# A hybrid mLSTM / attention layer on one core: key loads a unit earlier, input scaling on another engine, slots and operand planes moved

## The chip, the core and the metric

The kernel runs on one core of one Trainium2 chip. Its engines work side by side, each through its own queue in order: TensorE (PE, with its weight loads as PEld), VectorE (DVE), ScalarE (ACT), GpSimd (POOL) and SyncE (SP), which here issues nearly all DMAs. Instructions of different engines wait for each other through semaphores. The metric is the device time of one execution in microseconds, as a median of runs.

## What is computed

One encoder layer on x of 2048 tokens by 1024 channels, in f32. It is, cut to what matters:

```
h = rmsnorm(x, g_mix);  z = h @ w_in
split z: qk_m, v_m, o_m, i, f | q, k, v of the neighbourhood attention | q_mem | gate_pre
h_m   = mLSTM in both directions over (silu(conv(qk_m)), v_m, i, f), summed, normed, times sigmoid(o_m)
h_na  = attention of each of 32 x 64 grid points to its 8 x 16 neighbours, with a bias table
h_mem = attention to 256 memory tokens
y     = sum over branches of sigmoid(gate) * (branch @ w_proj)
x     = x + y @ w_out
x     = x + relu(rmsnorm(x, g_ffn) @ w_up)^2 @ w_down
```

## The kernel before

**Precision.** A product in f32 is made of three matmuls: each operand is split into a high and a low plane, and high x high, high x low and low x high are summed (`mm3`, lines 241 to 243). ACT writes the high plane and DVE the low one: L185 and L186 for weights, L447 and L448 for inputs, L1365 and L1366 for the gates' operands.

**Blocks, groups, ticks.** Phase 1 walks four blocks (0 to 3) of 512 tokens. `block_a` runs the groups of one block in order: q and k of the neighbourhood attention; its v with q_mem; the convolved mLSTM q and k (4 groups); mLSTM v (4 groups); in blocks 1 and 2 four early gates; the output gate o (4 groups); in block 3 eight more gates. A group is 24 matmuls of 128x512, and after every 6 of them `tick()` runs: it takes one job off a list and advances the side streams by a step. The neighbourhood attention (`na_stream`), the memory attention and the q/k normalisation are such streams, so that their small matmuls lie between the large ones. TensorE's order is that of the program, written out by hand. The order of the other queues is made by a planner from priorities, which follow the program order; an instruction traced at `cur_priority + LATER` (60) counts as if it came later.

**Next block's inputs.** While one block is at work, `prep_x` loads a tile of 128 tokens of the next (already transposed, `xT`) and scales it by the gain `gmix` (a column for each of 8 slices) and by the reciprocal norms `rb` (a row), in eight DVE instructions (L428). `trans_x` then queues two jobs that split the tile into the planes of `hT`. There are two buffers for such tiles (tag `xt`). They are shared with `rms_x`, which loads the next block for its norms, and with `sums_down`.

**Sums of the down weights.** `sums_down` loads two 512 KB tiles of weights, makes four differences on DVE (L606) and stores them. There are 16 of these. `SUMS_1` says how many are made in each block of phase 1; the rest are made in `pair_gates`, in phase 3.

**Neighbourhood attention.** Its work is cut into units (group of query rows g, heads hg, half), each of four scores. `na_unit` fetches one: with half 0 it loads keys and queries in six DMAs (tiles `nak` and `naq`, two buffers each), with half 1 it uses the same ones. A score (`na_scores`) is one matmul (L1115), a minimum over scores and bias on DVE (L1118), the exponential on ACT (L1120), a reciprocal (L1122) and a scaling (L1123) on DVE, and a zero fill of the tile's end on POOL (L1126). Some ticks later TensorE transposes it (`na_transpose`, L1134), and after four heads `na_values` (L1148) multiplies with v. The tile for the scores has three buffers. The line that decides when a unit is fetched is:

```
            if todo and not fetched and (cur is None or cur["h"] > 0):
                last = self.na_unit(*todo.pop(0), last, 4 if cur else 8)
```

**Phase 2** runs the remaining gates of blocks 3 and 0 as 24-matmul groups, and the mLSTM (`ml_stream`) between them by ticks. Its 32 chunks (two directions in turn) start one in each slot; a slot has 3 or 4 ticks. From slot 16 on a chunk also adds the other direction's output, normalises, multiplies by the output gate and is transposed (L936 to L956). `load_raw` reloads the raw inputs of blocks 1 and 2 at a fixed gate.

**Phase 3** begins with the gates that are left when the mLSTM stream has ended. Beside them, one job a tick, `gate_operands` forms sums of the raw inputs (L1371) and splits them into planes (`X`). `pair_gates` then makes the remaining gates of blocks 1 and 2 in pairs, seven products for eight, followed by the merge, the output projection and the MLP in the same scheme.

Of the kernel before, what the change touches and what calls it, by code (L numbers as in the profile page):

```python
# [14 lines left out]
F32R = mybir.dt.float32r  # L15
BF16 = mybir.dt.bfloat16
AF = mybir.ActivationFunctionType
ALU = mybir.AluOpType
# [7 lines left out]
LOW, LATER, LATER_A, SOON = 100, 60, 60, 40  # L26
# [2 lines left out]
PAD = 256  # L29
EV = {1: 2, 2: 2, 3: 8}  # L30
XT = 2
PREP_V = 2
MEM_T, MEM_R = 6, 3
NA_LATER, NA_VALUES, NA_HOLD = {1: 5, 2: 5, 3: 4}, {1: 3, 2: 3, 3: 2}, 3
NAB = 4
# [4 lines left out]
NB = S // TB  # L40
# [6 lines left out]
SPILL = [0]  # L47
NA_AT = {1: (3,), 2: (1, 3), 3: (1, 2, 3)}
NA_RATE = {0: 1, 1: 2, 2: 2, 3: 2}
SUMS_1 = {0: 1, 1: 2, 2: 2, 3: 6}  # L50


def units(g):
# [31 lines left out]
class Body:  # L85
# [330 lines left out]
    def prep_x(self, gsrc=None, xt=None):  # L416

        if self.xorder:
            nc = self.nc
            b, t = self.xorder.pop(0)  # L420
            r0 = b * TB + t * 128
            if b == 0:
                self.xhs.append((self.load_norm(self.a["x"][r0:r0 + 128], self.gbc, gsrc, xt), t, False))
                return
            xt = self.x_tile(self.a["xT"][4 * b + t]).rearrange("p (k t) -> p k t", k=8)
            rb = self.rb[:, t * 128:(t + 1) * 128]
            for k in range(8):
                nc.vector.scalar_tensor_tensor(xt[:, k], xt[:, k], self.gmix[:, k:k + 1], rb, ALU.mult, ALU.mult)  # L428
            if b in GATES_3:
                self.store(self.scr["raw"][b][:, :, t * 128:(t + 1) * 128], xt)  # L430
            self.xhs.append((xt, t, True))
# [70 lines left out]
    def block_a(self, b):  # L502


        nc, a = self.nc, self.a
        hT = self.hT
        w = self.take(4)
        for i, t in enumerate(ORDER_0 if b == 0 else range(4)):
            if i == 0 or b == 0 and i < 3:
                self.trans_x()  # L510
            if b == 0 and i == MEM_R:
                self.mem_rms()
            p = self.tok_group(hT, w, t)
            z = self.t("zna", [128, 512], 4)
            nc.scalar.activation(z, p, AF.Copy)
            self.qkq.append(self.na_qk(b, t, z.rearrange("p (a b) -> p a b", b=32)))
        if b + 1 < NB:
            rms = self.rms_x(b + 1)
            self.jobs += [lambda: next(rms, None), None] * 10
        if b in SPILL:  # L520
            for k in range(8):
                self.jobs += [lambda k=k: self.store(self.scr["hT"][b][:, :, k], hT[:, :, k].bitcast(F32)), None]
        w = self.take(4)
        zif = self.t("zif", [128, 4, 16], 1)
        for t in range(4):
            p = self.tok_group(hT, w, t, slice(0, 256), 4)
            s = self.ev()[:, 0:256]
            nc.scalar.activation(s, p, AF.Copy)

            for half in range(2):  # L530
                for r in range(2):
                    p0 = r * 64 + half * 24
                    self.store(self.scr["vna"][half, 8 * b + 2 * t + r], s[p0:p0 + 40])
            self.done.add(("v", 4 * b + t))
            p = self.tok_group(hT, w, t, slice(256, 528), 4)
            z = self.t("zm", [128, 256], 4)
            nc.vector.tensor_copy(z, p[:, 0:256])
            nc.scalar.activation(zif[:, t], p[:, 256:272], AF.Copy)  # L538
            self.memq.append(self.mem_unit(b, t, z))
        self.jobs += [None, None, lambda: self.if_rows(b, zif)]  # L540
        if b == NB - 1:
            self.na_rate = 3
            self.mem_lanes[1] = (0,)
        gml = self.gbc[:, b % 2 * TB:(b % 2 + 1) * TB]
        sums, n = None, SUMS_1[b]

        def sum_step():
            nonlocal sums, n
            if sums is None and n:
                sums, n = self.sums_down(self.down_q.pop(0), self.x_tiles), n - 1  # L550
            sums = sums and next(sums, None) and sums

        for c in range(4):
            if c % 2:
                sum_step()
            self.conv(b, c, self.ch_group(self.take(1)[0], hT))
        w = self.take(4)
        for t in range(4):
            if t == PREP_V and b + 1 < NB and b not in GATES_3:
                self.prep_x()  # L560
            p = self.tok_group(hT, w, t)
            s = self.ev()
            nc.scalar.activation(s, p, AF.Copy)
            self.store(self.scr["v"][b][t * 128:(t + 1) * 128], s)
            if b == NB - 1:
                sum_step()
        if b in GATES_3:
            for j in range(EARLY):
                if j == EARLY - 2:
                    self.prep_x()  # L570
                self.gate(b, j)
                if j < 2:
                    sum_step()
        nc.sync.dma_start(gml, a["g_mlstm"])
        w = self.take(4)
        for t in range(4):
            if t:
                self.trans_x()
            if t < 3:
                self.prep_x()  # L580
            p = self.tok_group(hT, w, t)
            s = self.ev()
            nc.scalar.activation(s, p, AF.Tanh, scale=0.5)
            nc.vector.scalar_tensor_tensor(s, s, 1.0, gml, ALU.add, ALU.mult)
            self.store(self.scr["og"][b][t * 128:(t + 1) * 128], s)
        if b == NB - 1:
            for j in range(FIRST_3):
                if j == 2:
                    self.ml_logsig()
                self.gate(b, j)  # L590
                sum_step()
# [69 lines left out]
    def ml_stream(self):  # L661


        rows = self.ml_rows(0)
        for tick in range(START_2):
            if tick >= ROWS_2:
                next(rows, None)
            yield
        slot = 0
        dirs = [list(range(16)), list(range(15, -1, -1))]  # L670
        live = [[], []]
        when = {0: [3, 2], 1: [1], 2: [], 3: [3, 1, 2, 1, 2, 3, 1, 0]}
        d = 0
        while any(dirs) or any(live[0]) or any(live[1]):
            c = dirs[d].pop(0) if dirs[d] else None

            ticks = 3 if slot < 20 or slot >= 32 else 4
            if slot % 8 == 2 and slot < 24:
                rows = self.ml_rows(slot // 8 + 1)
            slot += 1  # L680
            live[d] = [None if c is None else self.ml_chunk(d, c)] + live[d][:3]
            for tick in range(ticks):
                for age in when[3 if tick == ticks - 1 else tick]:
                    if age < len(live[d]) and live[d][age]:
                        next(live[d][age], None)
                if tick < ticks - 1:
                    next(rows, None)
                yield
            if len(live[d]) == 4:
                live[d][3] = None  # L690
            d = 1 - d
# [310 lines left out]
    def na_stream(self):  # L1002
# [6 lines left out]
        while True:  # L1009
            if self.na_wait and self.na_tiles(self.na_wait[0]) <= self.done:  # L1010
                hold += 1
                if hold > NA_HOLD:
                    hold, g = 0, self.na_wait.pop(0)
                    todo += [(g, hg, half) for hg in range(2) for half in range(2)]
            if todo and not fetched and (cur is None or cur["h"] > 0):
                last = self.na_unit(*todo.pop(0), last, 4 if cur else 8)
                fetched.append(last)
                biases += [(last, h) for h in range(4)]
# [56 lines left out]
    def na_unit(self, g, hg, half, before, wait):  # L1075
# [2 lines left out]
        u = dict(g=g, hg=hg, half=half, nk=nr * 40, pts=[], h=0, wait=wait)  # L1078
        u["qk"] = before["qk"] if half else self.na_load_qk(g, hg, kr0, nr)
        u["kts"] = [(3 * i, min(3, nr - 3 * i)) for i in range((nr + 2) // 3)]  # L1080
        u["ho"] = before["ho"] if half else self.t("nho", [128, 2, 256], 1, F32R)
        u["bias"] = []
        self.na_v.append(u)
        self.na_load_v()
# [56 lines left out]

    def na_values(self, u):
        nc = self.nc
        g, hg, half, ho, kts, pts = (u[x] for x in ("g", "hg", "half", "ho", "kts", "pts"))
        po = self.ps("mx")[:, 0:128]
        for j, (r0, n) in enumerate(kts):
            for h in range(4):
# [148 lines left out]
    def phase_3(self):  # L1296
# [14 lines left out]
        nc.sync.dma_start(self.gbc, a["g_ffn"])  # L1311
        if self.raw is None:
            self.late_gates(lambda: self.raw is None)
        self.jobs += self.gate_operands()
        self.late_gates(lambda: True)
        while self.jobs:
            self.tick()
# [37 lines left out]
    def gate_operands(self, late=False):  # L1355
# [5 lines left out]
        def split(x, src):  # L1361
            for k in (0, 2):
                def job(k=k):
                    hi, lo = (X[x][:, l, k:k + 2] for l in range(2))
                    nc.scalar.activation(hi, src[:, k:k + 2], AF.Copy)  # L1365
                    nc.vector.tensor_tensor(lo, src[:, k:k + 2], hi.bitcast(F32), ALU.subtract)  # L1366
                jobs.append(job)

        def op(out, x, y, how):
# [19 lines left out]
    def pair_gates(self, b0, b1, mix1):  # L1389
# [19 lines left out]
        for n, j in enumerate(pairs):  # L1409
# [14 lines left out]
            add(u3, u2, c21)  # L1424
            add(p5, u3, p5)
            out(p5, c2, j + 1)
            if sums:
                next(sums.pop(0), None)
            product(w, c12, "s4", "b22", False)
            add(u3, u2, c12)  # L1430
            out(u3, c2, j)
# [5 lines left out]
            if slots is None:  # L1437
                while self.jobs:
                    self.tick()
                slots = self.p_h.tile([128, 4, 2, 1024], F32, name="sG", tag="hT", bufs=1)  # L1440
            for _ in range(1 + (n == 0)):
                if self.down_q:
                    q = self.down_q.pop(0)
                    load = lambda q, s=slots[:, q % 4]: self.sums_load(q, s)
# [328 lines left out]
```

## Time and profile before

| | us |
|---|---|
| median of 3 runs | 2931.28 |
| lowest and highest run | 2923.46, 2934.57 |
| profiled execution | 2925.4 |
| its span, first to last instruction | 2923.7 |
| PE, PEld busy | 2850.3, 2348.0 |
| DVE, ACT, POOL busy | 2086.1, 1219.6, 216.8 |

All later numbers of the trace are from the profiled execution. Times of day, as "at 354", are microseconds from the start of the span. A line of a timeline gives start, duration, engine, line of the kernel, operation, output<-inputs, shapes and, in brackets, how long the engine had been idle before it and what ended that. A line of a table by group gives the count, then busy time, the mean duration in ns, and the idle time before. The granted clock is the share of TensorE's full rate.

### The profile page before, as it was taken

Reading aid. Unit: us, or ns where it says so; the run is one execution under the profiler, and the core shown is the slowest. Engines: PE = TensorE matmul, PEld = TensorE weight load, DVE = VectorE, ACT = ScalarE, POOL = GpSimd, SP = SyncE. Lnnn points to the kernel's source line nnn. Section 1 sums busy time; section 2 is a strip of 40 time slices with the busy share of each in tenths; the row PEclk is TensorE's granted clock in tenths of the full one; section 3 lists DMA queues with packets and bytes.
Section 4 is the critical chain, followed back from the end, with each engine's and each line's share of the span. In section 5 each row is a group of like instructions: output and inputs, shape, how many; then the busy total and the mean of one; then the engine's idle time right before and its main releaser. Section 6 shows DMA issues by size and latency. Waiting matters only on the chain.

```text
span 2923.7 us, 41742 instructions
## 1 busy us (share of the span) xinstructions
PE 2850.3 (97%) x14908; PEld 2348.0 (80%) x14908; DVE 2086.1 (71%) x3586; ACT 1219.6 (42%) x2326; POOL 216.8 (7%) x382
## 2 busy tenths in 40 slices
PE   8999999998999989999999999999999999999999
PEld 7787787787777768888888888888888888888887
DVE  5768768787645668657598888566786988885666
ACT  6556556455443445442243334533312433344331
POOL 4130030120012320000000000000000000000000
PEclk9999999999999999999999999999999999999999
DMA  7877968878887895738344446756864444466554
GB/s 263 252 246 224 288 210 256 270 224 253 282 273 250 275 321 195 274 112 267 123 142 155 154 159 206 246 189 222 308 200 125 141 158 146 154 241 212 190 191 160
DMA packets 341488, 625.42 MB, mean 214 GB/s; under 512 B 29120, under 2 KB 150912, under 8 KB 340768
## 3 DMA queue, kind: packets, MB, share of 16 engines
q1 hardware_dynamic: 341280, 622.76, 65.3%
q8 instruction: 117, 1.92, 0.3%
q14 instruction: 91, 0.75, 0.1%
HBM read 446.03 MB, written 176.62 MB: 213 GB/s over the span
## 4 chain that ended last, share of the span: by engine, by line
PE 83%; DVE 6%; DMA 6%; issue 2%; ACT 2%; SPq 1%; POOL 1%; DVEq 0%; ACTq 0%; POOLq 0%
PE mm L241 26%; PE mm L243 25%; PE mm L242 25%; DVE ws L186 1%; PE tr L1134 1%; DMA nak<-s_ks 1%; ACT ws L185 1%; PE pn L903 1%; PE mx L1148 1%; PE mx L1115 1%; DVE cy L711 1%; DMA wr<-in_w_units_dram 1%; DMA wb<-s_w 0%; PE mm L1536 0%; PE pn L906 0%
## 5 line engine op out<-in xcount | busy, mean ns | idle before, releaser
L241 PE MATMUL mm<-X,ws 128*128 128x512 f32 x1032 | 401.8, 389 | 0.0
L243 PE MATMUL mm<-X,ws 128*128 128x512 f32 x1032 | 401.5, 389 | 0.0
L242 PE MATMUL mm<-X,ws 128*128 128x512 f32 x1032 | 401.5, 389 | 0.0
L211 ACT ACTIVATE ws<-wr 128x512 fp32r<-128x512 f32 x294 | 176.8, 628 | 280.6 <-PE mm L243 181.7
L186 DVE TENSOR_TENSOR ws<-wr,ws 128x1024 fp32r<-128x1024 f32 (+1 forms) x160 | 196.7, 1236 | 84.5 <-ACT ws L185 79.1
L243 PE MATMUL mm<-X 128*128 128x512 f32 x616 | 239.7, 389 | 0.0
L242 PE MATMUL mm<-X 128*128 128x512 f32 x616 | 239.6, 389 | 0.0
L241 PE MATMUL mm<-X 128*128 128x512 f32 x616 | 239.6, 389 | 0.0
L241 PE MATMUL mm<-ws,hT 128*128 128x512 f32 (+2 forms) x640 | 233.6, 365 | 5.3 <-ACT zif L538 2.9
L243 PE MATMUL mm<-ws,hT 128*128 128x512 f32 (+2 forms) x640 | 226.8, 354 | 1.9 <-DVE hT L448 1.9
L242 PE MATMUL mm<-ws,hT 128*128 128x512 f32 (+2 forms) x640 | 226.1, 353 | 0.2 <-DVE ws L186 0.2
L243 PEld LDWEIGHTS mm<-X,ws 128*128 128x128 f32 x1032 | 193.7, 188 | 40.2
L242 PEld LDWEIGHTS mm<-X,ws 128*128 128x128 f32 x1032 | 193.7, 188 | 40.2
L241 PEld LDWEIGHTS mm<-X,ws 128*128 128x128 f32 x1032 | 193.8, 188 | 40.0
L185 ACT ACTIVATE ws<-wr 128x1024 fp32r<-128x1024 f32 (+1 forms) x160 | 168.3, 1058 | 103.3 <-PE mm L243 88.6
L212 DVE TENSOR_TENSOR ws<-wr,ws 128x512 fp32r<-128x512 f32 x294 | 198.2, 688 | 1.4
L1658 ACT ACTIVATE X<-X 128x1024 fp32r<-128x1024 f32 x109 | 115.7, 1062 | 198.2 <-DMA X<-s_t 79.2
L1659 DVE TENSOR_TENSOR X<-X 128x1024 fp32r<-128x1024 f32 x109 | 133.0, 1223 | 74.6 <-ACT X L1658 74.2
L1685 DVE TENSOR_TENSOR acc<-acc,mm 128x512 f32<-128x512 f32 x192 | 126.5, 684 | 65.4 <-PE mm L243 65.3
L241 PE MATMUL mm<-hT,ws 128*128 128x512 f32 x384 | 157.2, 409 | 0.7 <-ACT ev L626 0.7
L243 PE MATMUL mm<-hT,ws 128*128 128x512 f32 x384 | 150.6, 392 | 0.0
L242 PE MATMUL mm<-hT,ws 128*128 128x512 f32 x384 | 150.4, 392 | 0.0
(310 smaller groups left out, 6240.8 us busy)
## 6 DMA issues: line engine op xcount, KB each, us to landing
wr<-in_w_units_dram SPq DMA_DIRECT2D x276, 512.0 KB
s_s<-u SPq DMA_DIRECT2D x32, 1024.0 KB
s_g<-ev SPq DMA_DIRECT2D x96, 256.0 KB
ev<-s_g SPq DMA_DIRECT2D x96, 256.0 KB
s_a<-u SPq DMA_DIRECT2D x96, 256.0 KB
X<-s_s SPq DMA_DIRECT2D x45, 512.0 KB
nab<-in_rpb_dram SPq DMA_DIRECT2D x96, 220.0 KB
X<-s_a SPq DMA_DIRECT2D x32, 512.0 KB
```

The costliest lines, as they stand in the source:

```text
L185: nc.scalar.activation(w[:, 0], raw, AF.Copy)
L186: nc.vector.tensor_tensor(w[:, 1], raw, w[:, 0].bitcast(F32), ALU.subtract)
L211: nc.scalar.activation(hi, src, AF.Copy)
L212: nc.vector.tensor_tensor(lo, src, hi.bitcast(F32), ALU.subtract)
L241: mm(out, lhs[0], rhs[0], start=first, stop=False)
L242: mm(out, lhs[0], rhs[1], start=False, stop=False)
L243: mm(out, lhs[1], rhs[0], start=False, stop=last)
L711: nc.vector.scalar_tensor_tensor(y, z[:, k:k + n], self.cw[:, c, k:k + 1], y, ALU.mult, ALU.add)
L903: mm(pn[h % 2][:, h // 2], pt[:, h], v1[:, h], start=h < 2, stop=first)
L1658: nc.scalar.activation(hi, src, AF.Copy)
L1659: nc.vector.tensor_tensor(lo, src, hi.bitcast(F32), ALU.subtract)
L1685: nc.vector.tensor_tensor(c, c, p, ALU.add)
```

## The change

Six things, most of them one line each.

- **Keys.** A unit is fetched also when one is in hand already, if another is running; and when none is in hand, at once. The output tile `nho` is made in `na_values` instead of with the unit.
- **Scaling.** `prep_x` uses two GpSimd instructions over the whole tile of 128x1024 instead of eight on DVE.
- **When tiles are prepared.** In block 0 before value groups 0 and 2 (before: 2 only); in blocks 1 and 2 before early gates 0 and 2 (before: 2 only). In the output-gate groups the remaining two are jobs behind the split jobs of groups 1 and 2 (before: calls ahead of groups 0, 1 and 2).
- **Sums.** Blocks 1 and 2 make one each (before: two). `pair_gates` makes seven instead of five: up to two a pair in the first three pairs.
- **mLSTM slots.** Three ticks in slots 0 to 15 and from 32 on, four in 16 to 31 (before: three up to 19).
- **Operand planes.** `gate_operands` begins four empty jobs later, and its splits are traced at a priority 60 later.

```
-PREP_V = 2
+PREP_V = (0, 2)
-SUMS_1 = {0: 1, 1: 2, 2: 2, 3: 6}
+SUMS_1 = {0: 1, 1: 1, 2: 1, 3: 6}
...
-            for k in range(8):
-                nc.vector.scalar_tensor_tensor(xt[:, k], xt[:, k], self.gmix[:, k:k + 1], rb, ALU.mult, ALU.mult)
+            for y in (self.gmix.unsqueeze(2), rb.unsqueeze(1)):
+                nc.gpsimd.tensor_tensor(xt, xt, y.to_broadcast([128, 8, 128]), ALU.mult)
...
-            if t == PREP_V and b + 1 < NB and b not in GATES_3:
+            if t in PREP_V and b + 1 < NB and b not in GATES_3:
                 self.prep_x()
...
-                if j == EARLY - 2:
+                if j % 2 == 0:
                     self.prep_x()
                 self.gate(b, j)
-                if j < 2:
-                    sum_step()
...
             if t:
                 self.trans_x()
-            if t < 3:
-                self.prep_x()
+                if t < 3:
+                    self.jobs.append(self.prep_x)
...
-            ticks = 3 if slot < 20 or slot >= 32 else 4
+            ticks = 3 if slot < 16 or slot >= 32 else 4
...
-            if todo and not fetched and (cur is None or cur["h"] > 0):
+            if todo and (not fetched or len(fetched) == 1 and cur):
...
-        u["ho"] = before["ho"] if half else self.t("nho", [128, 2, 256], 1, F32R)
...
-        g, hg, half, ho, kts, pts = (u[x] for x in ("g", "hg", "half", "ho", "kts", "pts"))
+        g, hg, half, kts, pts = (u[x] for x in ("g", "hg", "half", "kts", "pts"))
+        if half == 0:
+            self.nho = self.t("nho", [128, 2, 256], 1, F32R)
+        ho = self.nho
...
-        self.jobs += self.gate_operands()
+        self.jobs += [None] * 4 + self.gate_operands()
...
+                    prio = self.tc.cur_priority
+                    self.tc.cur_priority = prio + LATER
                     nc.scalar.activation(hi, src[:, k:k + 2], AF.Copy)
                     nc.vector.tensor_tensor(lo, src[:, k:k + 2], hi.bitcast(F32), ALU.subtract)
+                    self.tc.cur_priority -= LATER
...
-            if sums:
-                next(sums.pop(0), None)
+            for _ in range(1 + (n < 3)):
+                if sums:
+                    next(sums.pop(0), None)
...
-            for _ in range(1 + (n == 0)):
+            for _ in range(1 + (n < 3)):
```

## The prediction

> **What bounds the kernel now.** I read the busy times first, then stretches of the span, then who TensorE waited for, then the timeline at each wait. In the stretches the columns are the length, then busy time and instructions of PE, PEld, DVE, ACT and POOL, the granted clock, the DMA share and GB/s.
>
> ```profile
> span 2923.7 us, 41742 instructions
> PE 2850.3 (97%) x14908; PEld 2348.0 (80%) x14908; DVE 2086.1 (71%) x3586; ACT 1219.6 (42%) x2326; POOL 216.8 (7%) x382
> ...
> 546.00:776.00 230.00, 219.07 (x1564) 179.02 (x1564) 170.11 (x419) 125.45 (x288) 32.52 (x76) 0.99 0.84 252
> ...
> 946.00:1000.00 54.00, 48.97 (x310) 38.96 (x309) 37.43 (x78) 21.70 (x83) 17.36 (x28) 1.00 0.81 247
> 1000.00:1142.50 142.50, 127.22 (x702) 103.65 (x701) 97.23 (x166) 66.89 (x209) 32.42 (x49) 0.95 0.85 280
> 1142.50:2917.00 1774.50, 1773.30 (x7880) 1467.33 (x7879) 1301.75 (x1814) 632.73 (x896) 0.00 (x0) 1.00 0.55 187
> ```
>
> TensorE sets the end. From 1142.5 on, where the MLP and the paired gates lie, it idles 1774.50 - 1773.30 = 1.2 us: nothing is to be had there, and anything added there that DVE or the DMA can absorb is free. The other idle time lies before 1142.5. The change adds and removes no matmul, so it can only act on these gaps and on what a gap does to the clock: the granted clock is 0.95 in 1000 to 1142.5, where 15.3 us are idle, and 1.00 behind it. I price a gap with its clock loss. Over the whole span 2923.7 - 2850.3 = 73.4 us are idle, so no edit to waiting can bring more than that and the clock.
>
> **The keys.** An attention unit is four scores (L1115); two units share one set of keys, loaded by six DMAs. Before, a unit is fetched when the current one has made a score and none is in hand. These four scores are each the first on a new set of keys; the bracket is TensorE's idle time and what the profile blames.
>
> ```profile
> 340.49 0.44 PE L1115 MATMUL mx<-nak,naq 96*128 96x440 f32 x1 [2.27 <-issue]
> 670.11 0.64 PE L1115 MATMUL mx<-nak,naq 96*128 96x440 f32 x1 [4.44 <-DMA nak<-s_ks]
> 700.63 0.44 PE L1115 MATMUL mx<-nak,naq 96*128 96x440 f32 x1 [1.48 <-DMA nak<-s_ks]
> 749.01 0.38 PE L1115 MATMUL mx<-nak,naq 96*128 96x320 f32 x1 [1.25 <-DMA cz<-s_fg]
> ```
>
> Then the last key DMA of the set used at 670.11, and the stretch around it:
>
> ```profile
> 662.38 0.31 SPq L1072 DMA_DIRECT2D nak<-s_ks  x1
> ...
> 650.00:675.00 25.00, 19.83 (x149) 15.29 (x146) 13.97 (x42) 10.75 (x27) 0.96 (x6) 0.93 1.03 294
> ```
>
> Two of the four have another label, but all fall on the first score of a pair of units, so I count them as the same wait: 2.27 + 4.44 + 1.48 + 1.25 = 9.44 us. The clock adds (1 - 0.93) x 25 = 1.75 us in the stretch that holds the largest. The last key DMA of that set was issued at 662.38 and the score began at 670.11, 7.7 us later, with the DMA engines full (1.03). After the change the fetch happens when one unit is in hand and another runs, so the load starts while the first unit of the pair before runs, not the second: more than one unit, five scores, sooner. 670.11 and 700.63 are the first scores of two sets that follow each other, eight scores in 30.5 us or 3.8 each, so the lead grows by an estimated 19 us, four times the largest wait. Two key tiles exist; the one needed was freed a score earlier, so SP shouldn't stand at these DMAs. V and bias loads keep their own counters, and the output tile moves to the values step. I take all of it: **-11.2 us** (bounds: -11.2, and 0 if the DMA engines are the limit, below).
>
> **The scaling on GpSimd.** Twelve token tiles are scaled. Before: eight DVE instructions each; after: two POOL passes over 128x1024.
>
> ```profile
> L428 DVE SCALAR_TENSOR_TENSOR xt<-xt,gmix,gbc 128x128 f32<-128x128 f32 x96 | 27.1, 347 | 9.2 <-DMA xt<-in_xT_dram 9.2
> L972 POOL TENSOR_TENSOR zna<-zna,rs 128x512 f32<-128x512 f32 x16 | 18.3, 1145 | 1.3
> L1233 POOL TENSOR_TENSOR zm<-zm,rs 128x256 f32<-128x256 f32 x18 | 13.5, 752 | 1.4
> ```
>
> One wait of TensorE in DVE's order of work, the same later, and all waits of this kind (total, times, longest):
>
> ```profile
> 351.46 1.65 DVE L428 SCALAR_TENSOR_TENSOR xt<-xt,gmix,gbc 128x128 f32<-128x128 f32 x6
> 353.62 1.23 DVE L186 TENSOR_TENSOR ws<-wr,ws 128x1024 fp32r<-128x1024 f32 x1 [0.52 <-ACT ws L185]
> 354.77 0.61 DVE L428 SCALAR_TENSOR_TENSOR xt<-xt,gmix,gbc 128x128 f32<-128x128 f32 x2
> 355.29 1.22 DVE L186 TENSOR_TENSOR ws<-wr,ws 128x1024 fp32r<-128x1024 f32 x1
> 356.43 0.45 DVE L1123 TENSOR_SCALAR nsb<-nsb,sm 128x440 f32<-128x440 f32 x1
> ...
> 363.40 2.19 DVE L428 SCALAR_TENSOR_TENSOR xt<-xt,gmix,gbc 128x128 f32<-128x128 f32 x8
> ...
> PE tr L1134 <- DVE nsb L1123: 6.2, 3, 2.2
> ```
>
> The stretches that hold the three waits:
>
> ```profile
> 350.00:375.00 25.00, 20.90 (x140) 16.60 (x142) 22.14 (x57) 15.05 (x30) 1.96 (x7) 0.93 0.96 318
> 525.00:550.00 25.00, 22.45 (x158) 17.93 (x157) 17.97 (x52) 11.96 (x24) 0.66 (x5) 0.95 0.90 294
> ```
>
> DVE is freed of 27.1 us. At 356.43 the softmax scaling (L1123), on which the transposes L1134 wait, stands behind eight L428 and two L186; from 363.40 eight L428 run in one piece before the next. The third wait, in 525 to 550, I read the same way. Eight take 1.65 + 0.61 = 2.26 us, over the longest wait of 2.2, so all 6.2 us go. Clock: (1 - 0.93) x 25 + (1 - 0.95) x 25 = 3.0 us. **-9.2 us**; bounds: 0 if L186 or a late load keeps L1123 late, -9.2.
>
> POOL gains 24 passes. From 752 ns at 256 columns and 1145 at 512, 1.54 ns a column: an estimated 1145 + 512 x 1.54 = 1.93 us a pass, 46 us in all on an engine that is 7% busy. A tile takes 3.9 us in place of 2.26, so 1.6 us later. Two of a block's four tiles now start much earlier (first and third value group, or first and third early gate), and the two sums dropped from blocks 1 and 2 no longer hold their buffers. The other two are emitted in the output-gate group, each two token groups ahead of its split into planes: ACT may stand there, and behind it PSUM evictions. For the three block changes that is six tiles at 0 to 1.6 us: 0 to 9.8; I take the middle, **+4.8 us**, as nothing here shows POOL in that place.
>
> **mLSTM slots.** Slots 16 to 19 get a fourth tick each, six more gate matmuls. TensorE's work is unchanged; gates only move. I match these slots with the stretch just before 946, and the idle time comes after: 54.00 - 48.97 = 5.0 us in 946 to 1000, where second-half chunks load saved scores and old outputs. More time per slot lets their loads keep up. Bounds -5.0 to +5.0 (a shift can as well move a wait); I take **-2 us**.
>
> The largest wait of all is later:
>
> ```profile
> PE tr L951 <- DVE h L947: 16.5, 8, 7.3
> ```
>
> It falls beside the reload of the raw inputs (128 x 8192 floats, 4 MB). That reload comes at a fixed gate; the slot's phase there is the same, one slot earlier, so I leave it at 0, but keep a gain for a rival.
>
> **Operand planes and sums.** The stream ends four ticks, one gate, later, so phase 3 starts one gate nearer to its first product on X.
>
> ```profile
> 1118.04 3.91 ACT L1365 ACTIVATE X<-raw 128x1024 fp32r<-128x1024 f32 x4 [1.97 <-DMA s_g<-ev]
> ...
> 1139.39 2.36 DVE L1366 TENSOR_TENSOR X<-raw,X 128x1024 fp32r<-128x1024 f32 x2
> ...
> 1142.52 0.39 PE L241 MATMUL mm<-X,ws 128*128 128x512 f32 x1
> ```
>
> Before, splitting started when X's space came free (1118.0) and the last plane was ready at 1141.8, 0.8 us ahead of the first product; that plane is used by the third. A matmul of the last stretch above takes 1774.5 / 7880 = 0.225 us, so a product of 12 takes 2.7 us, and that plane's slack is 0.8 + 5.4 = 6.2 us. A gate is 24 matmuls, 5.4 us. So one gate later it fits by 0.8 us; the cover is thin. Lower priority lets weights pass first. Bounds 0 to 5.4; I take **+1.4 us**. The two sums moved behind 1142.5 cost DVE eight instructions of 128x512 (0.68 us for that form, below) and 4 MB of DMA (eight tiles of 512 KB) where TensorE idles 1.2 us: 0.
>
> **Sum:** -11.2 - 9.2 + 4.8 - 2 + 1.4 = -16.2 us against the profiled execution's 2925.4 (span 2923.7 and 1.7 around it). The median of three runs is 2931.28, 5.9 above that execution; the same difference from it gives **2915 us**.
>
> **POOL beside DVE.**
>
> ```profile
> 1035.58 1.09 POOL L855 TENSOR_SCALAR_AFFINE_SELECT de<-de 128x512 f32<-128x512 f32 x1
> 1036.10 1.11 DVE L936 TENSOR_TENSOR h<-h,hf 128x512 f32<-128x512 f32 x1
> ...
> 1103.03 0.68 DVE L936 TENSOR_TENSOR h<-h,hf 128x512 f32<-128x512 f32 x1
> ```
>
> The same DVE form took 0.68 us alone and 1.11 beside a POOL pass, 0.43 more. The Trainium skill, SBUF — State Buffer, "Who interferes with whom", says that a DVE instruction with two SBUF inputs and a GpSimd one that reads SBUF exclude each other for the whole instruction, whichever comes first; the row agrees in sign, and by that rule a pass of 1.93 us could hold DVE for all of it.
>
> **Rivals.**
> 1. *The transfers are the limit.* DMA share is 1.03 at 650 to 675 and 0.96 at 350 to 375; earlier keys push weights and biases back, and TensorE waits for these. For: that share. Against: the stretch around has 0.84. The 11.2 us stay: 2926 us.
> 2. *POOL holds DVE.* 24 passes at 0.43 us are 10 us, at 1.93 us 46 us, against 27.1 freed. Against: most passes will meet instructions with a PSUM operand or none. At the upper end the 9.2 us stay: 2924 us.
> 3. *POOL's queue becomes the wait (slower).* Each score's zero padding is a POOL memset that must precede its transposes:
>
> ```profile
> 350.98 0.13 POOL L1126 MEMSET nsb<- 128x40 f32 x1 [3.30 <-PE tr L1134]
> ```
>
>    It follows the transposes three scores back. POOL had idled 3.30 us since the memset before (0.13 us), so scores lie 3.4 us apart here, and it has three of them, 10.3 us, until its own transposes. A tile's passes (3.9 us) ahead of it, and all the time that they stand for their load or scale row, delay it; over 10.3 us TensorE waits. If all twelve tiles do so at the size of the gaps above (2.1 us, and 1.75 of clock), 12 x 3.85 = 46 us: 2915 - 4.8 + 46 = 2956 us. Against: L428 waited only 9.2 us for all its loads.
> 4. *More goes.* With more filler in slots 30 and 31 most of the 16.5 us before L951 goes too, say 12: 2903 us.
> 5. *Nothing moves,* as the planner of the other queues puts the passes where they hold as much: 2931 us.
>
> **Chances.** Forecast 0.56 (own range 2904 to 2924), rival 1 0.13, 2 0.08, 3 0.08, 4 0.13, 5 0.02. About 0.5% (14.7 us) is what a measurement of this kernel can tell from no change. Below 2916.6: 0.42 of the forecast's 0.56 and rival 4, 0.55. Above 2946: rival 3, 0.08. Within: 0.37. The range 2898 to 2932 leaves out rival 3 and the ends of the rest.
>
> **What would show it.** Right: first scores on new keys without idle time; no L428 on DVE and no wait of L1134 for L1123 over 1 us; POOL some 46 us busier; span to the first product on X 15 to 20 us shorter, and nothing changed behind. Wrong: L1134 behind L1126, ACT's hT behind POOL's xt for microseconds, DMA waits before other instructions, idle time before the first products on X.

## The result: 0.7% slower, and the profile after

The changed kernel took 2951.55 us (median of 5, 2947.68 to 2956.56) beside 2932.19 for the one before (5 runs). The ratio is 1.0072, 95% interval 1.0052 to 1.0091: about 21 us slower, where the prediction had 16 us less. The page of the profiled execution (2953.93 us) begins:

```profile
span 2952.2 us, 41677 instructions
PE 2861.8 (97%) x14908; PEld 2353.6 (80%) x14908; DVE 2092.6 (71%) x3490; ACT 1218.8 (41%) x2326; POOL 268.4 (9%) x406
```

Two stretches of it, one late in the first phase and the whole of the last (columns as in the prediction):

```profile
725.00:750.00 25.00, 18.61 (x148) 14.70 (x150) 14.52 (x38) 13.76 (x29) 0.66 (x5) 0.86 0.69 193
...
1174.00:2946.00 1772.00, 1769.01 (x7855) 1461.93 (x7854) 1304.76 (x1821) 625.43 (x887) 0.00 (x0) 1.00 0.56 189
```

TensorE idles 2952.2 - 2861.8 = 90.4 us, against 73.4 before, and it is busy 11.5 us longer with the same 14908 matmuls, at a mean granted clock of 0.990 against 0.993. Behind 1174 it idles 3.0 us, so the loss isn't there. It lies ahead of it, and 725 to 750 shows it at its worst: 6.4 us idle in 25, the clock at 0.86, and the DMA engines at a share of 0.69, by no means full.

POOL gained 51.6 us (46 were expected). DVE was freed of 27.1 us of scaling, yet its busy time went up by 6.5. That is the first surprise. The second is in the list of what TensorE waited for (total, times, longest):

```profile
PE tr L1131 <- DVE nsb L1120: 15.2, 7, 6.4
PE tr L949 <- DVE h L945: 12.5, 7, 3.9
...
PE mx L1112 <- DVE sm L1115: 5.4, 3, 3.1
```

In the changed kernel L1112 is the score, L1115 the minimum with its bias on DVE, L1120 the scaling, L1131 the transposes, L1103 the bias load, L1069 and L1070 the key loads. The wait that was to go, 6.2 us before, is 15.2. What the keys' edit was to remove is gone, though: the first scores on the four sets of keys that TensorE waited for before have no idle time in front. One other first score has, at 657.46, and the profile puts that down to DVE's minimum:

```profile
351.12 0.45 PE L1112 MATMUL mx<-nak,naq 96*128 96x440 f32 x1
...
657.46 0.74 PE L1112 MATMUL mx<-nak,naq 96*128 96x440 f32 x1 [3.05 <-DVE sm L1115]
...
687.43 0.44 PE L1112 MATMUL mx<-nak,naq 96*128 96x440 f32 x1
...
718.73 0.45 PE L1112 MATMUL mx<-nak,naq 96*128 96x440 f32 x1
...
750.77 0.39 PE L1112 MATMUL mx<-nak,naq 96*128 96x320 f32 x1
```

So the keys come in time, and something behind the score is late. The largest gap shows what. First TensorE, the score and the transposes that end the gap; then SP's queue; then DVE:

```profile
730.27 0.45 PE L1112 MATMUL mx<-nak,naq 96*128 96x440 f32 x1
...
745.55 0.87 PE L1131 MATMUL tr<-ident,nsb 128*120 128x128 f32 x3 [6.39 <-DVE nsb L1120]
```

```profile
725.93 0.43 SPq L1070 DMA_DIRECT2D nak<-s_ks  x1
736.51 0.36 SPq L181 DMA_DIRECT2D wr<-in_w_units_dram  x1
736.91 0.43 SPq L1069 DMA_DIRECT2D naq<-s_qs  x1
737.39 0.43 SPq L1070 DMA_DIRECT2D nak<-s_ks  x1
737.86 0.90 SPq L1103 DMA_DIRECT2D nab<-in_rpb_dram  x2
```

```profile
735.26 1.22 DVE L186 TENSOR_TENSOR ws<-wr,ws 128x1024 fp32r<-128x1024 f32 x1 [1.35 <-ACT ws L185]
...
742.79 0.61 DVE L1115 CUSTOM_DVE_ANT_0 nsb<-mx,nab 128x440 f32<-128x440 f32 x1 [1.29 <-DMA nab<-in_rpb_dram]
```

SP stood from 726.4 to 736.5 at a weight load, which needs a raw weight tile that DVE's L186 gave back at 736.48. Behind the weight load come the last two key loads of the next set, and behind those the bias of a score that TensorE had made at 730.27. The bias is issued 7.6 us after its score, the minimum runs at 742.79, 12.5 us after the score, and everything after it waits. Before, the same weight load stood in the same place among the same keys, and nothing urgent was behind it (SP's queue of the kernel before; L1106 is the bias load):

```profile
718.72 0.35 SPq L181 DMA_DIRECT2D wr<-in_w_units_dram  x1
719.12 0.43 SPq L1071 DMA_DIRECT2D naq<-s_qs  x1
719.59 0.43 SPq L1072 DMA_DIRECT2D nak<-s_ks  x1
720.07 0.43 SPq L1106 DMA_DIRECT2D nab<-in_rpb_dram  x1
```

By count, the bias at 720.07 is that of the first score on these new keys (number 112, made at 725.0): 4.9 us ahead. In the changed kernel the bias in this place is number 108, four scores earlier. That is what the two-ahead fetch did: a unit has four biases, and the next set's keys went into the queue one unit sooner, ahead of them. Over all 128 scores, 6 biases are issued after their score where it was 1 before, and 45 minima start over 5 us after it where it was 15.

### The profile page after: what moved, and what is told of

Its sections match the earlier page's. It is cut to its first block, busy times and chain, and to the rows that moved or that the text cites. A ratio compares the mean times of both kernels' runs of the same rounds, so it can differ in the third digit from the quotient of the medians.

```text
span 2952.2 us, 41677 instructions
## 1 busy us (share of the span) xinstructions
PE 2861.8 (97%) x14908; PEld 2353.6 (80%) x14908; DVE 2092.6 (71%) x3490; ACT 1218.8 (41%) x2326; POOL 268.4 (9%) x406
## 4 chain that ended last, share of the span: by engine, by line
PE 82%; DVE 6%; DMA 6%; issue 2%; ACT 2%; SPq 1%; POOL 1%; DVEq 0%; ACTq 0%; POOLq 0%
PE mm L241 25%; PE mm L242 25%; PE mm L243 25%; PE tr L1131 1%; DVE ws L186 1%; DMA nab<-in_rpb_dram 1%; PE pn L901 1%; DMA wr<-in_w_units_dram 1%; ACT ws L185 1%; PE mx L1148 1%; PE mx L1112 1%; PE pn L904 1%; DVE nsb L1115 1%; PE mm L1540 0%; DMA og<-s_o 0%
## 5 line engine op out<-in xcount | busy, mean ns | idle before, releaser
L186 DVE TENSOR_TENSOR ws<-wr,ws 128x1024 fp32r<-128x1024 f32 (+1 forms) x160 | 203.5, 1280 | 85.8 <-ACT ws L185 85.5
```

Source lines behind the costliest of these rows:

```text
L186: nc.vector.tensor_tensor(w[:, 1], raw, w[:, 0].bitcast(F32), ALU.subtract)
```

## The experiments

Ratios are to the kernel before on the same chip, with 95% intervals; us is the ratio's distance from 1 times 2930. By these intervals a difference between two runs is uncertain by 4 to 7 us. How late a tile is in e14, e16 and e17 is the mean in the trace, from the end of DVE's scaling to the end of what was put behind it.

| run | keys | scaling | other | ratio | us |
|---|---|---|---|---|---|
| the change | two ahead | GpSimd | | 1.0072 (1.0052-1.0091) | +21.1 |
| e1 | old | GpSimd | | 1.0026 (1.0015-1.0037) | +7.6 |
| e2 | two ahead | DVE | | 1.0073 (1.0058-1.0087) | +21.4 |
| e3 | old | DVE | | 0.9971 (0.9961-0.9981) | -8.5 |
| e4 | old | GpSimd | else as before | 1.0059 (1.0046-1.0071) | +17.3 |
| e5 | two ahead | DVE | else as before | 1.0128 (1.0108-1.0147) | +37.5 |
| e6 | two ahead | DVE | as e5, biases on GpSimd's queue | 0.9978 (0.9968-0.9988) | -6.4 |
| e7 | old | DVE | before, biases on GpSimd's queue | 0.9994 (0.9983-1.0006) | -1.8 |
| e8 | old | DVE | before, with slots and planes | 0.9997 (0.9989-1.0006) | -0.9 |
| e9 | old | GpSimd | as e1, raw stores on GpSimd's queue | 1.0015 (1.0005-1.0025) | +4.4 |
| e10 | two ahead | DVE | as e2, biases on GpSimd's queue | 0.9930 (0.9915-0.9945) | -20.5 |
| e11 | old | DVE | as e3, raw stores on GpSimd's queue | 0.9954 (0.9941-0.9968) | -13.5 |
| e12 | two ahead | GpSimd | the change, both on GpSimd's queue | 1.0015 (1.0005-1.0025) | +4.4 |
| e13 | old | DVE | as e3, passes that nobody reads | 1.0056 (1.0042-1.0070) | +16.4 |
| e14 | old | DVE | as e3, tile 1.5 us later | 0.9968 (0.9955-0.9980) | -9.4 |
| e15 | old | GpSimd | as e1, passes in halves | 1.0019 (1.0008-1.0030) | +5.6 |
| e16 | old | DVE | as e3, tile 3.6 us later | 0.9991 (0.9981-1.0001) | -2.6 |
| e17 | old | DVE | as e3, tile 5.6 us later | 0.9980 (0.9969-0.9990) | -5.9 |

**Which part costs.** e1 and e2 undo one part of the change each, the first and the second hunk below; e5 and e4 do the same part alone in the kernel before, the same lines the other way round.

```diff
-if todo and (not fetched or len(fetched) == 1 and cur):
+if todo and not fetched and (cur is None or cur["h"] > 0):
...
-for y in (self.gmix.unsqueeze(2), rb.unsqueeze(1)):
-    nc.gpsimd.tensor_tensor(xt, xt, y.to_broadcast([128, 8, 128]), ALU.mult)
+for k in range(8):
+    nc.vector.scalar_tensor_tensor(xt[:, k], xt[:, k], self.gmix[:, k:k + 1], rb, ALU.mult, ALU.mult)
```

> The changed kernel with the old fetch condition: a unit is fetched only when none is in hand and the running one has made a score; all else as changed. Theory A (keys first, biases late: the two-ahead fetch puts six key loads and two V loads into SP's queue ahead of bias loads that are due sooner, and the min on DVE waits for the bias) expects about 2938 us, 13 below the changed kernel, the 6.39 us gap at 739 gone, and gaps at first scores on new keys (some 9 us) back. Theory B (GpSimd scaling: its passes keep DVE out and its queue is late) expects 2950 us, within 4 of the changed kernel. Theory C (the new times at which tiles are prepared and sums are made) expects 2950 too.

> The changed kernel with the scaling back on DVE, eight instructions a tile, at the changed kernel's times of preparation; all else as changed. Theory A expects about 2950 us, within 4 of the changed kernel. Theory B expects about 2936 us: the 3.59 us gap at 173 gone, DVE instructions with two SBUF inputs back at their usual length there (L582 0.69 us instead of 2.75). Theory C expects 2950. If A and B each hold for a part, this and the kernel with the old fetch lose about 8 and 12 us of the 20.

> The kernel before with one edit: the two GpSimd passes in place of eight DVE instructions a tile, at the old times. Theory B expects 2938 to 2945 us, slower than before by 6 to 13. Theory A expects the kernel before's 2932 or a little less, since DVE is freed of 27 us. Theory C: 2932.

> The kernel before with one edit: the two-ahead fetch (and the output tile taken at the values step, which it needs). Theory A expects 2940 to 2947 us, slower than before, with bias loads issued after their score had begun and a gap of several us in block 3. Theory B and C expect the 2920 that the prediction's term of -11 gives.

e1 is what theory A expected, with no bias issued after its score and 15 minima over 5 us behind theirs, as many as before. e5 is far beyond what A expected: the keys' edit alone costs 37 us. e4 is above the top of what theory B had. e2 was a miss for B: with the two-ahead fetch in place, taking the scaling off GpSimd brings nothing. So A and B both hold; as I read it they act on the same thing, the chain from a score to its transposes on DVE, and where biases make it late the other delay is hidden. e5, with neither GpSimd scaling nor new times, has the same two rows as the changed kernel, and larger:

```profile
PE tr L1133 <- DVE nsb L1122: 17.5, 9, 6.5
...
PE mx L1150 <- DVE sm L1117: 8.1, 3, 4.8
```

**What the rest of the change is worth.** e3 is the change with both hunks above undone; e8 is the kernel before with the slots and the operand planes of the change, their lower priority too:

```diff
-ticks = 3 if slot < 20 or slot >= 32 else 4
+ticks = 3 if slot < 16 or slot >= 32 else 4
...
-self.jobs += self.gate_operands()
+self.jobs += [None] * 4 + self.gate_operands()
```

> The changed kernel with the old fetch condition and with the scaling back on DVE: what is left of the change is when tiles are prepared, which sums are made where, the mLSTM slots and the operand planes. If keys and scaling hold all of the loss, it lies within 4 us of the kernel before. If the new times themselves cost what the kernel with only the old fetch condition still had above the kernel before (7.6 us), it is 5 to 10 us slower than before. If they gain and the passes on GpSimd cost as much as they did at the old times (17 us), it is some 9 us faster than before.

> The kernel before with two edits: slots 16 to 19 of the mLSTM get four ticks, and the operand planes begin four ticks later at a lower priority. The prediction's terms give -0.6 us; all theories of the loss expect within 4 us of the kernel before, and all of its difference behind the first phase.

e8 can't be told from no change. e3 is 8.5 us faster than before: the new times of preparing, with the sums moved, bring some 7.6 us, by subtraction; no run has them alone. The row that the scaling on GpSimd was to clear is all but cleared by them, on DVE (of e3):

```profile
PE tr L1131 <- DVE nsb L1120: 2.0, 2, 1.3
```

**Queue or transfers.** The same bytes, as early, with one thing changed: the queue that issues the biases. e6 is e5 with this edit, e7 the kernel before with it.

```diff
-self.nc.sync.dma_start(bias[:, :u["nk"]], self.a["rpb"][pat, u["half"], u["hg"] * 4 + h, :, :u["nk"]])
+self.nc.gpsimd.dma_start(bias[:, :u["nk"]], self.a["rpb"][pat, u["half"], u["hg"] * 4 + h, :, :u["nk"]])
```

> The kernel before with the two-ahead fetch, and the bias loads issued from GpSimd's queue instead of SP's. Theory A1 (SP's queue: four biases of the running set stand behind the next set's keys and the weight load among them, while the data itself would be there in time): the 37 us that the fetch alone cost shrink to under 12 above its control (the kernel before with the biases on GpSimd), the min on DVE starts within 5 us after its score everywhere, and no bias is issued after its score. Theory A2 (the transfers themselves: earlier keys take the DMA engines from biases and weights): 25 us or more above its control, since the same bytes move as early.

> The control: the kernel before with only the bias loads issued from GpSimd's queue. Both theories expect within 10 us of the kernel before; the gaps at first scores on new keys (9.4 us) stay, or shrink a little where SP no longer stands at a bias ahead of keys.

e6 is 4.6 us below its control and 43.9 below e5. Theory A1 holds, A2 falls: not the transfers but the place in SP's queue. No bias is issued after its score in e6, as A1 had it, against 10 in e5. One part of A1's text was too strong: the minimum still starts over 5 us after 11 of e6's 128 scores, but that is against 54 in e5 and 15 before. The row of e6 that answers to the 17.5 us above:

```profile
PE tr L1133 <- DVE nsb L1122: 2.1, 3, 1.3
```

e7 missed a part of its text: the gaps at first scores on new keys don't stay. Of the four in the prediction one is left, with the old fetch:

```profile
669.34 0.70 PE L1115 MATMUL mx<-nak,naq 96*128 96x440 f32 x1 [2.71 <-DMA nak<-s_ks]
```

So most of that wait, too, came with the biases in SP's queue and not with the fetch alone. Yet e7 can't be told from no change: 9.4 us of gaps became 2.7, and the time moved by 1.8 us, inside an interval of 3.4 either way.

The Trainium skill, DMA: Bandwidth & Descriptors, "Issuing engines are not separate DMA queues", says that all issuers' transfers share the same 16 engines and that spreading them saves only the time to issue, which is usually small. No run here speaks against the first half. The second leaves out what made these 44 us: a load that waits for its tile holds up every later load of its issuer, and another issuer's loads pass it.

**Why GpSimd costs 16 us.** e1 and e3 differ only in the scaling: 7.6 + 8.5 = 16.1 us. Three causes: SP stands at the raw stores until the passes end (B3); the passes exclude DVE (B1); the tile is later, and ACT stands at its first copy (L447). For B3 SP's timeline had a case: ahead of these eight stores SP issued nothing for some 45 us in all in e1, 27.9 in e3.

e9 is e1, e11 is e3 with these stores on GpSimd's queue; e12 is the whole change with them and the biases there.

```diff
-self.store(self.scr["raw"][b][:, :, t * 128:(t + 1) * 128], xt)
+for k in (0, 4):
+    nc.gpsimd.dma_start(self.scr["raw"][b][:, k:k + 4, t * 128:(t + 1) * 128], xt[:, k:k + 4])
```

> The changed kernel with the old fetch condition, and with the raw copies of the scaled tiles stored from GpSimd's queue, right behind the passes, instead of from SP's. Theory B3 (SP stands at these stores until the slower passes end, 44.8 us in the kernel with the old fetch condition against 27.9 with the scaling on DVE, and weights, biases and keys stand behind) expects most of the 16 us between those two to go: 2920 to 2925 us where before is 2930. Theory B1 (passes exclude DVE's instructions with two SBUF inputs; DVE was freed of nothing) expects 2934 to 2940, as with SP's queue left alone.

> The control for the stores: the changed kernel with the old fetch condition, the scaling on DVE, and the raw copies stored from GpSimd's queue. B3 expects a small gain on the same kernel with the stores on SP (its stand there was 27.9 us): 2914 to 2920 us where before is 2930. B1 expects 2920.

> The changed kernel whole, with two queues repaired: bias loads and raw stores are issued from GpSimd's queue. If the order in SP's queue is all of the loss, 2913 to 2918 us where before is 2930, what the prediction had. If the passes' exclusion of DVE holds a part, or biases now stand behind passes, 2925 to 2935.

Both kernels gain 3 to 5 us from it, and the difference between them stays: 4.4 + 13.5 = 17.9. B3 falls as the cause. e12, with both queues repaired, is still slower than before, so SP's order isn't all of the loss. It is 24.9 us above e10 (below), which has the scaling on DVE; that is more than 16.1, and biases that stand behind the passes in GpSimd's queue may hold a part, which no run shows.

For the exclusion, the rows of DVE and POOL in the changed kernel, block 0:

```profile
169.85 3.00 DVE L448 TENSOR_TENSOR hT<-xt,hT 128x512 fp32r<-128x512 f32 x2
...
172.84 2.75 DVE L582 SCALAR_TENSOR_TENSOR ev<-ev,gbc 128x512 f32<-128x512 f32 x1
...
176.55 1.28 DVE L448 TENSOR_TENSOR hT<-xt,hT 128x512 fp32r<-128x512 f32 x2
```

```profile
170.40 1.90 POOL L428 TENSOR_TENSOR xt<-xt,gmix 128x1024 f32<-128x1024 f32 x1 [6.12 <-DMA xt<-in_xT_dram]
172.38 2.67 POOL L428 TENSOR_TENSOR xt<-xt,gbc 128x1024 f32<-128x1024 f32 x1
```

Two L448 take 1.28 us alone and 3.00 beside the first pass. L582, 0.69 us in e3 (below), starts 0.5 us into the second pass and ends 0.5 us behind it, having taken 2.75 us. Over the whole kernel, L582's group (busy us, mean ns, then idle time before) and the busy times on the page, first of e3:

```profile
L582 DVE SCALAR_TENSOR_TENSOR ev<-ev,gbc 128x512 f32<-128x512 f32 x16 | 11.0, 687 | 1.6 <-ACT ev L581 1.6
```

```profile
PE 2844.1 (98%) x14908; PEld 2341.3 (80%) x14908; DVE 2084.6 (71%) x3586; ACT 1218.0 (42%) x2326; POOL 211.8 (7%) x382
```

Then of e1:

```profile
L582 DVE SCALAR_TENSOR_TENSOR ev<-ev,gbc 128x512 f32<-128x512 f32 x16 | 16.5, 1029 | 1.5 <-ACT ev L581 1.5
```

```profile
PE 2853.7 (97%) x14908; PEld 2348.9 (80%) x14908; DVE 2086.2 (71%) x3490; ACT 1216.2 (41%) x2326; POOL 269.8 (9%) x406
```

DVE lost 27.1 us of work (96 instructions) and is as busy as before: 2086.2 - (2084.6 - 27.1) = 28.7 us of its busy time is standing.

DVE instructions with one tile as input (and a column of scalars) stand as well, among them the scaling that a score's transposes wait for. In e4 (L584 and L1123 are L582 and L1120 here, and take 0.69 and 0.45 us alone), at the longest of these waits:

```profile
369.43 2.52 POOL L428 TENSOR_TENSOR xt<-xt,gmix 128x1024 f32<-128x1024 f32 x1 [5.26 <-DMA xt<-in_xT_dram]
372.03 2.67 POOL L428 TENSOR_TENSOR xt<-xt,gbc 128x1024 f32<-128x1024 f32 x1
```

```profile
370.23 2.27 DVE L584 SCALAR_TENSOR_TENSOR ev<-ev,gbc 128x512 f32<-128x512 f32 x1
372.42 2.52 DVE L1123 TENSOR_SCALAR nsb<-nsb,sm 128x440 f32<-128x440 f32 x1
```

```profile
375.09 1.08 PE L1134 MATMUL tr<-ident,nsb 128*120 128x128 f32 x4 [3.61 <-DVE nsb L1123]
...
PE tr L1134 <- DVE nsb L1123: 7.9, 3, 3.6
```

The last row is e4's total for the wait that was to go: 7.9 us, 6.2 before, with no L428 left on DVE. L1123's 128 instructions took 65.2 us there and 55.8 before.

The last runs part the standing from the later tile. e13 adds the first hunk to e3, behind DVE's scaling; e16 adds the second, and e17 the same with 7 memsets:

```diff
+for k in (0, 4):
+    for y in (self.gmix.unsqueeze(2)[:, k:k + 4], rb.unsqueeze(1)):
+        s = self.t("zna", [128, 512], 4).rearrange("p (k t) -> p k t", k=4)
+        nc.gpsimd.tensor_tensor(s, xt[:, k:k + 4], y.to_broadcast([128, 4, 128]), ALU.mult)
...
+s = self.t("zna", [128, 512], 4)
+c, one = xt[:, :, 0:1], self.ones[:, 0:8].unsqueeze(2)
+nc.gpsimd.tensor_tensor(s[:, 0:8].unsqueeze(2), c, one, ALU.mult)
+for _ in range(4):
+    nc.gpsimd.memset(s, 1.0)
+nc.gpsimd.tensor_tensor(c, c, s[:, 0:8].unsqueeze(2), ALU.mult)
```

e14 is like e17, but both products are of the tile with ones, so the memsets hang on nothing; e15 is e1 with the passes over four of the eight 128-column parts at a time.

> The kernel with both edits undone (0.9971 of before), and after DVE's scaling of each tile four GpSimd passes over 128x512 into a scratch tile that nobody reads: two inputs in SBUF, about 4.3 us a tile, so the exclusion of DVE without a later tile. If exclusion is the cause, 8 us or more above that kernel (ratio to before 1.000 or more), and DVE busy 20 us or more longer. If the late tile is, within 4 us of it (0.9971 to 0.9985).

> The kernel with both edits undone, and after DVE's scaling of each tile a GpSimd chain that the copies into planes and the raw store wait for: one product of 8 columns, seven memsets of 128x512 in a scratch tile (0.52 us each by the rows of such a memset), one product of 8 columns, about 4.3 us. The tile is as late as by the passes, or later by DVE's own 2.3 us, and there is almost nothing that reads two inputs beside DVE. If the late tile is the cause, 8 us or more above the kernel with both edits undone, with ACT's copy waiting for it; if exclusion is, within 4 us of it (0.9971 to 0.9985), and DVE busy unchanged.

> The changed kernel with the old fetch condition (1.0026 of before) and each GpSimd pass cut in two halves of 128x512, the first half of a tile finished first. Exclusion by long single passes expects a part of the 16 us back, 5 us or more (1.001 or less), since DVE gets its turn after 1.1 us rather than 1.9 to 3.3. A late tile, and exclusion by the sum of all passes, expect within 4 us of 1.0026, since the whole tile is done no sooner.

> The kernel with both edits undone, and after DVE's scaling of each tile a GpSimd chain that cannot be taken apart: a product of 8 columns into a scratch tile, four memsets of 128x512 over it, a product of 8 columns of the tile with it. The tile is about 2.7 us later than DVE's scaling, as by the passes, and nothing long that reads two inputs runs beside DVE. If the late tile is the cause of the 16 us, 8 us or more above the kernel with both edits undone (ratio to before 1.000 or more); if exclusion is, within 4 us of it (0.9957 to 0.9985).

> The same with seven memsets: the tile about 4.3 us later than DVE's scaling, more than by the passes. If the late tile is the cause, 16 us or more above the kernel with both edits undone; if exclusion is, within 5 us of it (up to 0.9988), and DVE's busy time unchanged at about 2085 us.

e13, passes that nobody waits for, costs 24.9 us above e3. The busy times on its page and its scaling group (347 ns each before, 597 here):

```profile
PE 2857.5 (97%) x14908; PEld 2350.0 (80%) x14908; DVE 2123.4 (72%) x3586; ACT 1217.6 (41%) x2326; POOL 282.6 (10%) x430
```

```profile
L428 DVE SCALAR_TENSOR_TENSOR xt<-xt,gmix,gbc 128x128 f32<-128x128 f32 x96 | 51.3, 597 | 3.3 <-DMA xt<-in_xT_dram 3.3
```

DVE stands 2123.4 - 2084.6 = 38.8 us. Of this 51.3 - 27.1 = 24.2 us lie in the scaling itself, which makes each tile some 2 us later here too and isn't on DVE in the change. So e13 shows that passes which nobody waits for can cost as much time, but not the price in the change.

The passes make a tile 1.8 us later: from its first to its last instruction it takes 4.9 us in e1 and 3.1 in e3, in the mean of the twelve. e14's memsets ran outside the chain, so its tile is 1.5 us late and not 4.3; it costs nothing (0.9 us below e3). e16 and e17 make the tile later than the passes do; they cost 5.9 and 2.6 us above e3. e16 lies between the two expectations, e17 meets that of the exclusion. As the longer delay costs no more than the shorter, I read 0 to 6 us for the late tile, and the other 10 to 16 of the 16 for the exclusion. e15 is 2.0 us below e1, which can't be told from nothing: no gain from shorter passes is shown.

What DVE loses depends on what POOL does. In e17 POOL ran 45.0 us of memsets (the passes took 56.1 in e1), and DVE stayed at its 2085 (the memsets' group, then the page):

```profile
L433 POOL MEMSET zna<- 128x512 f32 x84 | 45.0, 536 | 4.5
```

```profile
PE 2853.9 (97%) x14908; PEld 2348.7 (80%) x14908; DVE 2085.9 (71%) x3586; ACT 1218.6 (42%) x2326; POOL 275.0 (9%) x490
```

That is as the Trainium skill has it (SBUF — State Buffer, "Who interferes with whom"): a DVE instruction with two SBUF inputs contends with a GpSimd one that reads SBUF, not with one that only writes it. L1123 in e4's rows, with one tile as input, goes beyond that sentence.

**The best version.** The change with the scaling on DVE and the biases on GpSimd's queue:

> The changed kernel with the scaling on DVE and the bias loads issued from GpSimd's queue; the two-ahead fetch stays. If the new times (-9.7 against before) and the two-ahead fetch with biases out of its way (-7) add up, 2913 us where before is 2930. If the two act on the same waits, 2918 to 2921.

2908.72 us, ratio 0.9930: 20.5 us faster than before, 5.6 more than the two gains add up to (8.5 and 6.4), which is within the noise. Its page:

```profile
span 2903.5 us, 41719 instructions
PE 2843.4 (98%) x14908; PEld 2341.2 (81%) x14908; DVE 2082.0 (72%) x3586; ACT 1220.3 (42%) x2326; POOL 285.8 (10%) x510
```

TensorE idles 60.1 us, 13.3 less than before.

## Why the prediction was wrong, point by point

The four terms of the result add up: keys 21.1 - 7.6 = +13.5, scaling +16.1, slots and planes -0.9, new times with the sums -8.5 + 0.9 = -7.6; together +21.1, against -16.2. They hold for this order of undoing: with the scaling put back first (e2), the scaling is worth nothing and the keys 21.4 + 8.5 = +29.9.

1. **Keys, -11.2 predicted, +13.5 found (+37.5 alone): the step that failed.** The working was "V and bias loads keep their own counters". They do, but they keep no queue of their own. I had only asked whether SP would stand at the moved loads (it hardly does, 3.3 us in all at L1070 against 3.7 before), and not what stands behind them: four biases of the running set, and between keys and biases a weight load that stands for 10 us. With the biases out of that queue the gain is there: e10 is 12.0 us below e3, though part of that may be the biases' own move (-1.8 in e7). The size was too large as well: e6 has no idle time at any first score on new keys, and is 6.4 us faster than before, not 11.2.
2. **Its bound, "0 if the DMA engines are the limit".** Wrong kind of bound: a transfer that is moved forward can cost more than it was to bring. Rival 1 had the right victims (weights and biases pushed back) and the wrong mechanism and price: the DMA share was 0.69 in the worst stretch.
3. **Scaling, -9.2 predicted.** The waits of L1134 for L1123 did hang on eight L428 standing in front, but on when they came, not on the engine: e3 has them on DVE and waits 2.0 us. Moving them to POOL freed no DVE time at all, and it didn't end the wait: in e4 it is 7.9 us, with L1123 itself standing beside a pass. Rival 2 (POOL holds DVE) named the mechanism and its rows showed it; I set its worst at "the 9.2 us stay", by weighing the freed time against the lost. The two are about equal (27.1 and 28.7), and still 16 us went. e4 lost 17.3 us at the old times, so it isn't that the new times had cleared the place already; as I read it, the standing fell on instructions that a score waits for, as in e4's rows.
4. **Later tiles, +4.8.** Not shown. e14, about as late as the passes make a tile, cost nothing; e16 and e17, later still, 5.9 and 2.6 us.
5. **POOL's time, 46 us.** 51.6 were added; the first pass in the changed kernel's rows above took the 1.9 us of the estimate, the second 2.67. Of the second passes 0.5 us more is their own (last section).
6. **Slots and planes, -0.6.** Measured -0.9, with an interval from -3.2 to +1.8, so neither confirmed nor refuted. **Sums, 0:** not measured apart from the new times; together -7.6, a gain that the sum didn't hold.
7. **Rival 3 (POOL's queue becomes the wait) was the one slower case,** and not what happened: transposes waited for DVE, and biases, not memsets, were late. The slower case that decided wasn't among the rivals. That rival 3's 2956 us lies near the measured 2951.55 is luck.

What stays open: how the 10 to 16 us of the exclusion are split between DVE's own standing and the tile that the standing makes late, and which of the new times brings the 7.6 us.

## What to carry to other kernels

Moving a load forward moves it ahead of something: list what stands behind it in its issuer's queue, and the loads in between that wait for a tile, before counting the wait that it removes. An engine with spare time is not free if DVE stands beside it, as here beside GpSimd's passes over SBUF: 56.1 us of passes in e1 cost DVE 28.7. Look for DVE instructions that take longer beside such a pass before counting the time that they free. Where two edits both make the same chain late, neither shows its whole price while the other is in place, so undo each and both.

## What was not expected of the hardware

GpSimd as an issuer of loads was cheap here: in e6, 128 bias loads took 70.2 us of it (548 ns each), and DVE's busy time didn't move (2087.8 us, 2086.1 before). Beside the passes DVE's weight subtraction L186 took 1320 ns in the mean (e9) where it takes 1237 without them (e11). And two passes of one shape differ in themselves: in e1 the shortest first pass, by a column for each slice, took 1.90 us, and a second pass, by a row, 2.39 with no DVE instruction beside it:

```profile
159.90 2.39 POOL L428 TENSOR_TENSOR xt<-xt,gbc 128x1024 f32<-128x1024 f32 x1
```
